# An earlier send-off of one block's row minima in forgetting attention, and another order of weight tiles in the output projection

## The chip, the cores and the metric

The kernel runs on one core of one Trainium2 chip. The metric is the time of one execution on the device, in microseconds (us); less is better. In the views below PE is TensorE (PEld its weight loads), DVE is VectorE, ACT is ScalarE, POOL is GpSimd and SP is SyncE, which only issues transfers here. ACT issues transfers too (ACTq).

## The reference

One inference step of a layer that runs two token mixers on the same input and merges them. What matters here is the attention of the 1024 prompt rows (16 heads of 64, eight pairs of heads), beside a decode step of 8 streams of 16 rows over a cache of 1024 rows, and the output projection with its LayerNorm:

```python
s = jnp.einsum('bqhd,bkhd->bhqk', q, k).astype(jnp.float32) * (A_HEADDIM ** -0.5)
bias = jnp.moveaxis(cq, 1, 2)[..., :, None] - jnp.moveaxis(ck, 1, 2)[..., None, :]
mask = jnp.arange(k.shape[1])[None, :] <= q_pos[:, None]
p = jax.nn.softmax(jnp.where(mask, s + bias, -jnp.inf), axis=-1)
return jnp.einsum('bhqk,bkhd->bqhd', p.astype(v.dtype), v)
...
u = gate_m * jnp.einsum('ble,ed->bld', y_m, w_br_m) + gate_a * jnp.einsum('ble,ed->bld', y_a, w_br_a)
out = jnp.einsum('bld,de->ble', u, w_out)
x_new = layer_norm(DN_ALPHA * x + out, ln_g, ln_b)
```

## The kernel before

The kernel is one long stream of fp32 matmuls on PE. Each operand is split into a high and a low part, and a product is three matmuls (high by high, high by low, low by high; lines 242 to 244). In the attention stage PE computes, for head pair `hp`, the four projections of the pair (v, gate, q, k; a result tile is called `d`), and while it does so the pair before it goes through its attention, a few instructions at a time, in the gaps between projection matmuls. The order of all engines is the order of the code there (a manual schedule). Where each attention step stands is fixed by the list `plan` in the function `pair`: an entry is a position on PE's way through the projections (in ticks of about 1 us), a cost, and the steps that are issued at it.

The keys run down the partitions of a score tile and the queries along it. The 1024 queries are four blocks of 256, j = 0 to 3; block j has 2j+2 key tiles, in `S[j]` (tiles `st_3`, `st_2`). Signs are turned, so that the softmax needs a minimum over the keys. For block 3 and block 2 the steps are:

- `scores` (PE) and the bias on ACT (line 833); `least` folds the minima on DVE; `mins` turns them into columns of the tile `ext` (DVE, lines 856 and 857);
- `share`: PE transposes `ext` (line 862, tile `acmb` for block 3, `acmc` for block 2), DVE reduces the row (`rowmb`, `rowmc`, line 865), SP writes the row to `mn_d` in DRAM (line 876), and when that has landed reads it back, spread over all partitions, into `mb_b` or `mb_c` (line 879). The write and the read are called the trip below;
- `less` subtracts it from the scores on DVE (line 888; block 3 in four pieces that read `mb_b`, block 2 in three that read `mb_c`), `weights` takes the exponential on ACT (line 893);
- `values` multiplies by v on PE into a PSUM tile `o`; DVE then multiplies the gate tile `gs` by it (line 907). Block 3's and block 2's `o` are the same PSUM bank, so `values(2)` on PE waits for line 907 of block 3 on DVE. In DVE's queue that instruction stands behind the three subtractions of block 2.

The decode rows run in the same list: `s_scores` (reads the cache tiles `kc`), `s_weights`, `turn_s` (PE transposes, line 929, copies `PTs` on ACT, lines 930 and 931), `s_values` (reads `vc`). `load` issues one 1 MB cache tile from ACT (line 792) into one of three buffers, in turn; `s_bias` loads `sb` from there too (line 940). An instruction of ACT that issues a load takes its turn in ACT's queue, and the load goes out when that turn has come and its buffer is free.

The output projection (line 1222 on) has eight weight row tiles of `w_out`. Tiles 0 and 1 come through the same ring as all weights before them (`wr`, split into `wh` on ACT, line 224, and `wl` on DVE, line 225). Tiles 2 to 7 (`wor`, `woh`, `wol`, lines 1227 to 1229) lie where buffers of the merge stage lay, so that their loads wait for the last addition of that stage (POOL, line 1210). For each of nine row tiles b and each half n the loop takes k = 0 to 7 in order, three matmuls each (lines 1253 to 1255), into one of eight PSUM banks. Here a scheduler, not the code, sets the order of the instructions on each engine: it takes the matmuls whose inputs it holds to be ready.

Of the kernel before, what the change touches and what calls it, by code (L numbers as in the profile page):

```python
# [147 lines left out]
def trunk_step(ctx: ExitStack, tc: tile.TileContext, I, O):  # L148
    nc = tc.nc
    ve, ac, po, te, sy = nc.vector, nc.scalar, nc.gpsimd, nc.tensor, nc.sync  # L150
# [16 lines left out]
    def bank(name):  # L167
        banks.append(banks.pop(0))
        return pt(banks[-1], name)

    def ch(c):
        return slice(c * CW, (c + 1) * CW)
# [142 lines left out]
    for c in range(NCH):  # L315
        for h in range(4):
            k = slice(2 * h, 2 * h + 2)
# [477 lines left out]
    def pair(hp, r):  # L795
# [223 lines left out]
        def last(i):  # L1019
# [15 lines left out]
            (18.6, 0.2, (share, "b", (3,)), (last, 4)),  # L1035
            (20.0, 3.4, (scores, 2, 2), (s_scores, 0)),
            (23.0, 0.0, (least, 2, 2), (mins, 2, 0, "c")),
            (25.6, 0.0, (s_weights, 0)),
            (26.8, 0.0, (less, 3, 0, 4), (less, 3, 1, 4)),
            (28.4, 0.2, (share, "c", (2,)), (weights, 3, 0, 4), (load, "v", hp, 0, 1), (load, "k", hp, 1, 0), (less, 3, 2, 4), (less, 3, 3, 4)),  # L1040
            (29.4, 0.0, (weights, 3, 1, 4)),
            (30.6, 0.0, (weights, 3, 2, 4)),
            (31.0, 1.2, (turn_s, 0)),
            (32.0, 0.0, (weights, 3, 3, 4)),
            (34.6, 0.0, (less, 2, 0, 3), (less, 2, 1, 3), (less, 2, 2, 3)),
            (35.2, 8.0, (values, 3), (sums, 3), (s_values, 0, 0), (s_values, 0, 1), (s_norm, 0)),
            (36.6, 0.0, (weights, 2, 0, 3)),
            (37.8, 0.0, (weights, 2, 1, 3)),
            (39.2, 0.0, (weights, 2, 2, 3), (load, "k", hp, 1, 1), (s_bias, 1)),
            (45.7, 4.4, (values, 2), (scores, 1, 0), (scores, 1, 1), (least, 1, 0)),  # L1050
            (46.0, 0.0, (load, "v", hp, 1, 0)),
            (49.4, 0.0, (least, 1, 1), (mins, 1, 1, "a")),
# [50 lines left out]
    with tc.manual_schedule():  # L1103
        load("k", 0, 0, 0)
        load("k", 0, 0, 1)
        load("v", 0, 0, 0)
        r = pair_dense(0)
        for hp in range(1, 8):
            flow.start(pair(hp - 1, r))
            r = pair_dense(hp)  # L1110
        flow.start(pair(7, r))
        for j in range(GATES_SSD, GATES_SSD + GATES_FOX):
            gate_dense(j, fp, "kv1", 3)
        flow.drain()
        for fn in lazy.pop("after"):
            fn()
# [100 lines left out]
    wo = []  # L1217
# [16 lines left out]
    for c in range(NCH):  # L1234
        uh = xp.tile([P, 8, CW], F32R, tag=f"xhi{c % 2}", name=f"uh{c}")
        ul = xp.tile([P, 8, CW], F32R, tag=f"xlo{c % 2}", name=f"ul{c}")
        xr = xp.tile([P, 3, D], F32, tag="xlo2", name=f"xres{c}")
        sy.dma_start(xr[:], I["xt"][3 * c * P:(3 * c + 3) * P].rearrange("(j p) d -> p j d", p=P))
        for k in range(8):
            ac.copy(uh[:, k, :], acc[:, k, ch(c)])  # L1240
            ve.tensor_tensor(ul[:, k, :], acc[:, k, ch(c)], uh[:, k, :].bitcast(F32), ALU.subtract)
        for j in range(3):
            b = 3 * c + j
            js = slice(j * P, (j + 1) * P)
            r = op.tile([P, D], F32, tag="r", name=f"r{b}", bufs=3)
            w = 512 if b < 8 else 256
            st = op.tile([P, 4, 6], F32, tag="st", name=f"st{b}", bufs=2)
            mv = op.tile([P, 4], F32, tag="mv", name=f"mv{b}", bufs=2)
            for n in range(D // w):
                ns = slice(w * n, w * n + w)  # L1250
                d = bank(f"out{b}_{n}")
                for k in range(8):
                    te.matmul(d[:, :w], uh[:, k, js], wo[k][0][:, ns], start=(k == 0), stop=False)  # L1253
                    te.matmul(d[:, :w], uh[:, k, js], wo[k][1][:, ns], start=False, stop=False)
                    te.matmul(d[:, :w], ul[:, k, js], wo[k][0][:, ns], start=False, stop=(k == 7))  # L1255
                ve.scalar_tensor_tensor(r[:, ns], xr[:, j, ns], DN_ALPHA, d[:, :w], ALU.mult, ALU.add)
                ve.bn_stats(st[:, n, :], r[:, ns])
            ve.bn_aggr(mv[:, 0:2], st[:, :D // w].rearrange("p n s -> p (n s)"))
            ac.activation(mv[:, 2:3], mv[:, 1:2], AF.Sqrt, bias=epst[:], scale=1.0)
            ve.reciprocal(mv[:, 2:3], mv[:, 2:3])  # L1260
            for n in range(2):
                ns = slice(512 * n, 512 * n + 512)
                ve.scalar_tensor_tensor(r[:, ns], r[:, ns], mv[:, 0:1], gb[:, 0, ns], ALU.subtract, ALU.mult)
                ve.scalar_tensor_tensor(r[:, ns], r[:, ns], mv[:, 2:3], gb[:, 1, ns], ALU.mult, ALU.add)
                sy.dma_start(O["y"][b * P:(b + 1) * P, ns], r[:, ns])
# [86 lines left out]
```

## Time and profile before

| | us |
|---|---|
| median of 3 runs | 2114.12 |
| lowest and highest | 2109.73, 2114.17 |
| profiled execution, its own time | 2111.51 |
| its span, first to last instruction | 2109.7 |
| PE busy in it | 2065.1 |

The profiled execution is 2.6 us below the median. PE is busy for 98% of the span, so that some 45 us can be won by taking waits away from PE, and the other engines count only where PE waits for them.

### The profile page before, as it was taken

Reading aid. Unit: us, or ns where it says so; the run is one execution under the profiler, and the core shown is the slowest. Engines: PE = TensorE matmul, PEld = TensorE weight load, DVE = VectorE, ACT = ScalarE, POOL = GpSimd, SP = SyncE. Lnnn points to the kernel's source line nnn. Section 1 sums busy time; section 2 is a strip of 40 time slices with the busy share of each in tenths; the row PEclk is TensorE's granted clock in tenths of the full one; section 3 lists DMA queues with packets and bytes.
Section 4 is the critical chain, followed back from the end, with each engine's and each line's share of the span. In section 5 each row is a group of like instructions: output and inputs, shape, how many; then the busy total and the mean of one; then the engine's idle time right before and its main releaser. Section 6 shows DMA issues by size and latency. Waiting matters only on the chain.

```text
span 2109.7 us, 36535 instructions
## 1 busy us (share of the span) xinstructions
PE 2065.1 (98%) x14495; PEld 1901.6 (90%) x14495; DVE 1331.3 (63%) x2252; ACT 822.9 (39%) x1662; POOL 625.9 (30%) x789
## 2 busy tenths in 40 slices
PE   8999999999999999999999999999999999999998
PEld 7999989999999998998888889888888999999987
DVE  7578777777777686415776766767767343181365
ACT  3444444443434444325445454454453342020220
POOL 1156564555556463500111121011110012113400
PEclk9999999999999999999999999999999999999999
DMA  5213242423233324333655655545565652153242
GB/s 167 80 54 118 78 135 77 125 76 118 82 117 92 111 83 138 129 136 115 199 169 180 199 169 171 186 164 198 169 203 157 217 193 97 50 184 95 79 175 80
DMA packets 110747, 283.07 MB, mean 134 GB/s; under 512 B 18040, under 2 KB 67184, under 8 KB 100336
## 3 DMA queue, kind: packets, MB, share of 16 engines
q1 hardware_dynamic: 98032, 199.46, 29.6%
q10 hardware_dynamic: 12544, 81.27, 11.6%
q8 instruction: 114, 1.87, 0.4%
q14 instruction: 57, 0.47, 0.1%
HBM read 228.89 MB, written 51.79 MB: 133 GB/s over the span
## 4 chain that ended last, share of the span: by engine, by line
PE 58%; DVE 22%; DMA 10%; ACT 5%; issue 2%; POOL 2%; SPq 0%; ACTq 0%; DVEq 0%; POOLq 0%
PE d L242 14%; PE d L244 13%; PE d L243 13%; DVE st L888 3%; DVE m L605 3%; PE s L828 2%; DMA mn_d<-rowmc 2%; DMA mn_d<-rowmb 2%; DMA ce<-ac_d 2%; PE o L903 2%; PE dq L242 2%; PE dq L243 2%; PE dq L244 2%; PE out L1253 2%; PE out L1255 2%
## 5 line engine op out<-in xcount | busy, mean ns | idle before, releaser
L242 PE MATMUL d<-xh,wh 128*128 128x384 f32 (+1 forms) x2328 | 820.1, 352 | 16.5 <-ACT xh L320 6.4
L244 PE MATMUL d<-xh,wl 128*128 128x384 f32 (+1 forms) x2328 | 781.5, 336 | 0.1
L243 PE MATMUL d<-xl,wh 128*128 128x384 f32 (+1 forms) x2328 | 780.4, 335 | 1.1 <-DVE xl L321 0.9
L242 PEld LDWEIGHTS d<-xh,wh 128*128 128x128 f32 (+1 forms) x2328 | 436.4, 187 | 58.1 <-issue 19.9
L243 PEld LDWEIGHTS d<-xl,wh 128*128 128x128 f32 (+1 forms) x2328 | 436.6, 188 | 4.4 <-DVE xl L321 2.4
L244 PEld LDWEIGHTS d<-xh,wl 128*128 128x128 f32 (+1 forms) x2328 | 435.7, 187 | 1.7 <-DVE wl L225 0.4
L222 POOL TENSOR_TENSOR wl<-wr,wh 128x1024 fp32r<-128x1024 f32 (+1 forms) x58 | 137.7, 2374 | 315.2 <-ACT wh L221 315.2
L221 ACT CAST wh<-wr 128x1024 fp32r<-128x1024 f32 (+1 forms) x73 | 75.8, 1038 | 201.7 <-PE d L243 163.4
L605 DVE TENSOR_SCALAR m<-ce,nacum 128x128 f32<-128x128 f32 x288 | 118.9, 454 | 48.0 <-DMA ce<-ac_d 47.7
L833 ACT ACTIVATE st<-s,ckt 128x256 f32<-128x256 f32 (+1 forms) x320 | 115.0, 465 | 34.2 <-PE s L828 32.1
L893 ACT ACTIVATE st<-st 128x1024 f32<-128x1024 f32 x80 | 84.0, 1061 | 90.9 <-DVE st L888 88.1
L225 DVE SCALAR_TENSOR_TENSOR wl<-wr,wh 128x1024 fp32r<-128x1024 f32 x50 | 61.8, 1235 | 59.7 <-ACT wh L224 59.6
L837 POOL TENSOR_TENSOR st<-st,mask_bf 128x256 f32<-128x256 f32 x64 | 58.7, 937 | 134.7 <-ACT st L833 134.7
L903 PE MATMUL o<-st,vt 128*64 128x256 f32 (+1 forms) x640 | 72.0, 374 | 13.7 <-DVE gs L907 13.3
L903 PEld LDWEIGHTS o<-st,vt 128*64 128x64 f32 x640 | 47.0, 140 | 39.2 <-ACT st L893 18.7
L778 POOL COPY knew<-kf 128x128 f32<-128x128 f32 x8 | 2.3, 290 | 237.6 <-ACT kf L775 237.6
L224 ACT ACTIVATE wh<-wr 128x1024 fp32r<-128x1024 f32 x50 | 52.8, 1056 | 50.6 <-PE d L243 45.9
L819 POOL MEMSET st<- 128x256 f32 x32 | 10.0, 312 | 205.6 <-PE s L828 153.5
L609 DVE TENSOR_TENSOR m<-m,cbm 128x384 f32<-128x384 f32 x96 | 70.2, 780 | 0.6
L607 ACT ACTIVATE ce<-ce 128x384 f32<-128x384 f32 (+1 forms) x96 | 46.8, 487 | 58.1 <-DVE m L605 58.1
L243 PE MATMUL d<-yb0l,wh 128*128 128x384 f32 x192 | 64.1, 334 | 0.0
L243 PE MATMUL d<-yb1l,wh 128*128 128x384 f32 x192 | 64.1, 334 | 0.0
(621 smaller groups left out, 3973.8 us busy)
## 6 DMA issues: line engine op xcount, KB each, us to landing
wr<-in_wt SPq DMA_DIRECT2D x96, 512.0 KB
kc<-in_cache_k ACTq DMA_DIRECT2D x32, 1024.0 KB
vc<-in_cache_v ACTq DMA_DIRECT2D x32, 1024.0 KB
ce<-ac_d SPq DMA_DIRECT2D x96, 192.0 KB
wr<-in_wbr SPq DMA_DIRECT2D x24, 512.0 KB
gate_d<-gate SPq DMA_DIRECT2D x48, 192.0 KB
sb<-cs_d ACTq DMA_DIRECT2D x16, 576.0 KB
yr<-ym_d SPq DMA_DIRECT2D x16, 576.0 KB
```

Source lines behind the costliest of these rows:

```text
L221: ac.copy(hi[:, :cols], raw[:, :cols])
L222: lazy.get("sub", po).tensor_tensor(lo[:, :cols], raw[:, :cols], hi[:, :cols].bitcast(F32), ALU.subtract)
L225: ve.scalar_tensor_tensor(lo[:, :cols], raw[:, :cols], scale, hi[:, :cols].bitcast(F32), ALU.mult, ALU.subtract)
L242: te.matmul(out, wh, xh, start=(k == 0), stop=False)
L243: te.matmul(out, wh, xl, start=False, stop=False)
L244: te.matmul(out, wl, xh, start=False, stop=(k == n - 1))
L605: ve.tensor_scalar(m[:, j, :], ce[:, j * P:(j + 1) * P], nacum[:, b, h:h + 1], 0.0, ALU.add, ALU.min)
L609: ve.tensor_tensor(m[:], m[:], cbms[c][:], ALU.mult)
L833: ac.activation(S[j][:, e, kb, q0:], ps2[:, e, 256 * x + q0:256 * x + 256], AF.Identity, bias=ckt[:, kb, 2 * hp + e:2 * hp + e + 1])
L888: ve.tensor_tensor(w, w, mb[j][:, :, None, :].to_broadcast([P, 2, k1 - k0, 256]), ALU.subtract)
L893: ac.activation(w, w, AF.Exp, scale=-1.0)
L903: te.matmul(o[64 * e:64 * e + 64, 256 * at + q0:256 * at + 256], vt[:, kb, 64 * e:64 * e + 64], S[j][:, e, kb, q0:256], start=(kb == 0), s ...
```

## The change

There are two edits. In `plan` the trip of block 2 (`share "c"`) is issued ahead of block 3's four subtractions instead of between the second and the third. Of the two cache loads that ACT issued between block 3's exponentials, `load v ... 0 1` goes ahead of them (ahead of `s_weights`) and `load k ... 1 0` behind the first exponential of block 2. The other positions move by a tick or less. In the output projection the loop over weight tiles runs 0, 2, 3, 4, 5, 6, 7, 1.

```diff
             (23.0, 0.0, (least, 2, 2), (mins, 2, 0, "c")),
+            (24.0, 0.0, (load, "v", hp, 0, 1)),
             (25.6, 0.0, (s_weights, 0)),
-            (26.8, 0.0, (less, 3, 0, 4), (less, 3, 1, 4)),
-            (28.4, 0.2, (share, "c", (2,)), (weights, 3, 0, 4), (load, "v", hp, 0, 1), (load, "k", hp, 1, 0), (less, 3, 2, 4), (less, 3, 3, 4)),
...
+            (28.8, 0.2, (share, "c", (2,)), (less, 3, 0, 4), (less, 3, 1, 4)),
+            (29.6, 0.0, (weights, 3, 0, 4), (less, 3, 2, 4), (less, 3, 3, 4)),
...
-            (36.6, 0.0, (weights, 2, 0, 3)),
...
+            (37.2, 0.0, (weights, 2, 0, 3), (load, "k", hp, 1, 0)),
...
-                for k in range(8):
+                for k in (0, 2, 3, 4, 5, 6, 7, 1):
                     te.matmul(d[:, :w], uh[:, k, js], wo[k][0][:, ns], start=(k == 0), stop=False)
                     te.matmul(d[:, :w], uh[:, k, js], wo[k][1][:, ns], start=False, stop=False)
-                    te.matmul(d[:, :w], ul[:, k, js], wo[k][0][:, ns], start=False, stop=(k == 7))
+                    te.matmul(d[:, :w], ul[:, k, js], wo[k][0][:, ns], start=False, stop=(k == 1))
```

PE's own order in the attention stage stays as it was, row for row. DVE in the second pair (pair 1), from block 2's minima to block 3's product with the gate, before:

```order
L857 TENSOR_REDUCE ext<-tm_2_11326 128x16
L488 SCALAR_TENSOR_TENSOR gs_11261<-gs_11261,d_0_11268 128x384
L888 TENSOR_TENSOR st_3_11033<-st_3_11033,mb_b 128x2x512 x2
L865 TENSOR_REDUCE rowmc_11367<-acmc_11365 16x32
L888 TENSOR_TENSOR st_3_11033<-st_3_11033,mb_b 128x2x512 x2
L488 SCALAR_TENSOR_TENSOR gs_11261<-gs_11261,d_1_11352 128x384
L888 TENSOR_TENSOR st_2_11180<-st_2_11180,mb_c 128x2x512 x3
L907 TENSOR_TENSOR gs_10354<-gs_10354,o_3_11432 128x256
```

The same stretch of DVE now:

```order
L857 TENSOR_REDUCE ext<-tm_2_11326 128x16
L488 SCALAR_TENSOR_TENSOR gs_11261<-gs_11261,d_0_11268 128x384
L865 TENSOR_REDUCE rowmc_11367<-acmc_11365 16x32
L888 TENSOR_TENSOR st_3_11033<-st_3_11033,mb_b 128x2x512 x4
L488 SCALAR_TENSOR_TENSOR gs_11261<-gs_11261,d_1_11352 128x384
L888 TENSOR_TENSOR st_2_11180<-st_2_11180,mb_c 128x2x512 x3
L907 TENSOR_TENSOR gs_10354<-gs_10354,o_3_11430 128x256
```

The reduction that starts block 2's trip has moved from behind two of the four subtractions to ahead of all four; nothing else has moved on DVE there.

ACT in the same pair, from the decode rows' exponential (line 968) to the load of `sb`, before:

```order
L968 ACTIVATE ps_0_11300,ssum_0_11302<-ps_0_11300,mns_0_11301 128x1152
L487 ACTIVATE gs_11261<-d_0_11268 128x384
L893 ACTIVATE st_3_11033<-st_3_11033 128x2x512
L792 DMA vc_0_1_11373<-in_cache_v 128x2048
L792 DMA kc_1_0_11375<-in_cache_k 128x2048
L893 ACTIVATE st_3_11033<-st_3_11033 128x2x512
L487 ACTIVATE gs_11261<-d_1_11352 128x384
L893 ACTIVATE st_3_11033<-st_3_11033 128x2x512
L930 COPY PTs_0_11395<-tps_0_11396 128x1024
L931 COPY PTs_0_11395<-tns_0_11397 128x128
L893 ACTIVATE st_3_11033<-st_3_11033 128x2x512
L893 ACTIVATE st_2_11180<-st_2_11180 128x2x512 x3
```

The same stretch of ACT now, from one row further up:

```order
L833 ACTIVATE st_2_11180<-s_2_2_11281,ckt 128x128 x2
L792 DMA vc_0_1_11329<-in_cache_v 128x2048
L968 ACTIVATE ps_0_11300,ssum_0_11302<-ps_0_11300,mns_0_11301 128x1152
L487 ACTIVATE gs_11261<-d_0_11268 128x384
L893 ACTIVATE st_3_11033<-st_3_11033 128x2x512 x2
L487 ACTIVATE gs_11261<-d_1_11352 128x384
L930 COPY PTs_0_11392<-tps_0_11393 128x1024
L931 COPY PTs_0_11392<-tns_0_11394 128x128
L893 ACTIVATE st_3_11033<-st_3_11033 128x2x512 x2
L893 ACTIVATE st_2_11180<-st_2_11180 128x2x512
L792 DMA kc_1_0_11496<-in_cache_k 128x2048
L893 ACTIVATE st_2_11180<-st_2_11180 128x2x512 x2
```

The load of `vc` now stands behind block 2's last scores, the load of `kc` behind the first exponential of block 2, and the copies `PTs` ahead of the last two exponentials of block 3 instead of ahead of the last one.

PE at the start of the output projection, from the merge stage's last matmul (`wh121`, `wl121` are tile 0, `wh122`, `wl122` tile 1, `woh2` tile 2; `out0_0` is half 0 of row tile 0), before:

```order
L244 MATMUL d123_2_20335<-yb1h2_19122,wl120_20179 128x384
L1253 MATMUL out0_0_20434<-wh121_20271,uh0_20411 128x512
L1254 MATMUL out0_0_20434<-wl121_20272,uh0_20411 128x512
L1255 MATMUL out0_0_20434<-wh121_20271,ul0_20412 128x512
L1253 MATMUL out0_1_20461<-wh121_20271,uh0_20411 128x512
L1254 MATMUL out0_1_20461<-wl121_20272,uh0_20411 128x512
L1253 MATMUL out0_0_20434<-wh122_20368,uh0_20411 128x512
L1255 MATMUL out0_1_20461<-wh121_20271,ul0_20412 128x512
```

PE now, at the end of its work on tile 0:

```order
L1254 MATMUL out3_1_20679<-wh121_20271,uh1_20629 128x512
L1255 MATMUL out3_1_20679<-wl121_20272,uh1_20629 128x512
L1256 MATMUL out3_1_20679<-wh121_20271,ul1_20630 128x512
L1254 MATMUL out0_0_20434<-woh2_20373,uh0_20411 128x512
L1254 MATMUL out0_1_20461<-woh2_20373,uh0_20411 128x512
L1255 MATMUL out0_0_20434<-wol2_20374,uh0_20411 128x512
```

Before, tile 1 comes up at the 6th matmul, and 41 matmuls with tiles 0 and 1 stand ahead of the first with tile 2; now 24 matmuls stand there, all with tile 0 (eight PSUM banks, three each).

## Rows read from the trace of the kernel before

**Rows 1.** The page, its first part: busy time, share of the span and instructions of each engine.

```profile
PE 2065.1 (98%) x14495; PEld 1901.6 (90%) x14495; DVE 1331.3 (63%) x2252; ACT 822.9 (39%) x1662; POOL 625.9 (30%) x789
```

**Rows 2.** The waits of PE over the whole program: what waited, for what, us in total, times, longest.

```profile
PE o L903 <- DVE gs L907: 13.3, 8, 2.6
...
PE acmc L862 <- DVE ext L857: 2.0, 5, 0.6
PE out L1253 <- ACT wh L224: 1.9, 1, 1.9
PE tns L929 <- DVE rowmc L865: 0.7, 3, 0.3
```

**Rows 3.** The chain of waits in pair 1, from block 3's trip to its product with the gate: start us, us, what.

```profile
1060.41 5.97 DMA mn_d<-rowmb
...
1066.40 3.72 DMA mb_b<-mn_d
...
1070.14 2.36 DVE st L888 x2
...
1072.54 0.31 DVE rowmc L865
...
1072.86 6.57 DMA mn_d<-rowmc
...
1079.45 3.31 DMA mb_c<-mn_d
...
1082.78 3.50 DVE st L888 x3
1086.27 0.34 DVE gs L907
```

**Rows 4.** The timeline of PE at `values(2)` of pairs 1, 4 and 5, the three longest of the eight waits: start us, us, line, operation, tiles, count, in brackets the idle time before and what ended it.

```profile
1086.75 2.60 PE L903 MATMUL o<-st,vt 128*64 128x256 f32 x24 [2.60 <-DVE gs L907]
...
1337.70 4.28 PE L903 MATMUL o<-st,vt 128*64 128x256 f32 x24 [2.24 <-DVE gs L907]
...
1422.39 3.08 PE L903 MATMUL o<-st,vt 128*64 128x256 f32 x18 [2.14 <-DVE gs L907]
```

**Rows 5.** Busy time by stretch, from the start of `values(2)` to the end of the score matmuls behind it, in pairs 1, 4 and 5: stretch, its length, busy us of PE, PEld, DVE, ACT and POOL with their counts, granted TensorE clock (1.00 is 2.4 GHz, 0.50 is 1.2 GHz), DMA share, GB/s.

```profile
1086.75:1090.93 4.18, 4.18 (x49) 3.50 (x49) 4.08 (x4) 2.12 (x4) 0.00 (x0) 1.00 0.71 261
1337.70:1343.53 5.83, 5.83 (x49) 4.48 (x49) 5.58 (x7) 2.65 (x5) 0.31 (x1) 0.71 0.70 237
1422.39:1428.16 5.77, 5.77 (x49) 4.51 (x49) 5.53 (x7) 2.65 (x5) 0.31 (x1) 0.70 0.68 236
```

**Rows 6.** The timeline of all engines in pair 1, columns as in rows 4. The ACT row of line 833 is block 2's last scores, those of line 893 would be exponentials of block 3 (the last is shown); `o` is `values(3)`.

```profile
1061.75 1.35 ACT L833 ACTIVATE st<-s,ckt 128x256 f32<-128x256 f32 x4 [0.36 <-PE s L828]
...
1069.35 0.54 DVE L488 SCALAR_TENSOR_TENSOR gs<-gs,d 128x384 f32<-128x384 f32 x1
1069.58 0.30 PE L862 MATMUL acmc<-ident,ext 128*128 128x128 f32 x1 [0.36 <-DVE ext L857]
...
1071.49 0.33 ACTq L792 DMA_DIRECT2D vc<-in_cache_v  x1
...
1073.56 0.47 ACT L487 ACTIVATE gs<-d 128x384 f32<-128x384 f32 x1
...
1075.44 1.00 ACT L930 COPY PTs<-tps 128x1024 f32<-128x1024 f32 x1
1076.30 3.46 PE L903 MATMUL o<-st,vt 128*64 128x256 f32 x32
...
1076.48 1.07 ACT L893 ACTIVATE st<-st 128x1024 f32<-128x1024 f32 x1
```

**Rows 7.** The chain of waits of the whole program: block 2's write in pair 0, and a write of a row of sums (8 KB) to DRAM at a time when ACT had no cache load under way.

```profile
989.97 5.13 DMA mn_d<-rowmc
...
1468.67 1.69 DMA rc_d<-rows
```

**Rows 8.** The timeline of all engines at the start of the output projection, columns as in rows 4: the merge stage's last addition, the loads of tiles 2 and 3, their conversions on ACT and DVE, and those of tile 7.

```profile
2004.98 1.95 POOL L1210 TENSOR_TENSOR acc<-acc,g 128x384 f32<-128x384 f32 x1 [1.68 <-DVE g L1209]
2006.96 0.81 SPq L1227 DMA_DIRECT2D wor<-in_w_out  x2
...
2011.09 2.23 ACT L1228 ACTIVATE woh<-wor 128x1024 fp32r<-128x1024 f32 x2 [6.28 <-issue]
2012.18 2.39 DVE L1229 SCALAR_TENSOR_TENSOR wol<-wor,woh 128x1024 fp32r<-128x1024 f32 x2 [6.12 <-ACT woh L1228]
...
2025.21 1.06 ACT L1228 ACTIVATE woh<-wor 128x1024 fp32r<-128x1024 f32 x1 [1.35 <-DMA wor<-in_w_out]
...
2026.30 1.22 DVE L1229 SCALAR_TENSOR_TENSOR wol<-wor,woh 128x1024 fp32r<-128x1024 f32 x1 [1.18 <-ACT woh L1228]
```

**Rows 9.** The timeline of PE at the start of the output projection, columns as in rows 4: the first matmul of it, the wait for tile 1, two matmuls that have 24 others between them, and the first with tile 2.

```profile
2001.61 0.39 PE L1253 MATMUL out<-wh,uh 128*128 128x512 f32 x1
...
2004.86 0.50 PE L1253 MATMUL out<-wh,uh 128*128 128x512 f32 x1 [1.94 <-ACT wh L224]
...
2007.38 0.40 PE L1253 MATMUL out<-wh,uh 128*128 128x512 f32 x1
...
2013.07 0.39 PE L1254 MATMUL out<-wl,uh 128*128 128x512 f32 x1
2013.29 1.30 PE L1253 MATMUL out<-woh,uh 128*128 128x512 f32 x5
```

More of the change, by code (lines that the diff above doesn't have):

```diff
@@ L1037, in pair @@
             (23.0, 0.0, (least, 2, 2), (mins, 2, 0, "c")),
+            (24.0, 0.0, (load, "v", hp, 0, 1)),
             (25.6, 0.0, (s_weights, 0)),
-            (26.8, 0.0, (less, 3, 0, 4), (less, 3, 1, 4)),
-            (28.4, 0.2, (share, "c", (2,)), (weights, 3, 0, 4), (load, "v", hp, 0, 1), (load, "k", hp, 1, 0), (less, 3, 2, 4), (less, 3, 3, 4)),
[L1041 to L1046, printed above, removed]
-            (36.6, 0.0, (weights, 2, 0, 3)),
-            (37.8, 0.0, (weights, 2, 1, 3)),
-            (39.2, 0.0, (weights, 2, 2, 3), (load, "k", hp, 1, 1), (s_bias, 1)),
+            (28.8, 0.2, (share, "c", (2,)), (less, 3, 0, 4), (less, 3, 1, 4)),
+            (29.6, 0.0, (weights, 3, 0, 4), (less, 3, 2, 4), (less, 3, 3, 4)),
+            (30.4, 0.0, (weights, 3, 1, 4)),
+            (31.2, 1.2, (turn_s, 0)),
+            (31.8, 0.0, (weights, 3, 2, 4)),
+            (33.2, 0.0, (weights, 3, 3, 4)),
+            (35.4, 0.0, (less, 2, 0, 3), (less, 2, 1, 3), (less, 2, 2, 3)),
+            (35.8, 8.0, (values, 3), (sums, 3), (s_values, 0, 0), (s_values, 0, 1), (s_norm, 0)),
+            (37.2, 0.0, (weights, 2, 0, 3), (load, "k", hp, 1, 0)),
+            (38.4, 0.0, (weights, 2, 1, 3)),
+            (39.8, 0.0, (weights, 2, 2, 3), (load, "k", hp, 1, 1), (s_bias, 1)),
             (45.7, 4.4, (values, 2), (scores, 1, 0), (scores, 1, 1), (least, 1, 0)),
```

## The prediction

> **What bounds the kernel.** I read the page's busy times first: PE is busy for 98% of the span [rows 1], so only time in which PE stands still can be won. The waits of PE say where that is [rows 2]: the largest is `values(2)` (line 903), 13.3 us in eight times, once per head pair, put down to line 907 on DVE; the output projection's wait for weight tile 1 (line 224) is 1.9 us, once. The timeline shows the three longest of the eight: 2.60, 2.24 and 2.14 us [rows 4]. The chain of waits says why they are there [rows 3]. In pair 1 `mb_b` lands (1066.40 + 3.72), DVE does two of block 3's subtractions (2.36), then the reduction to `rowmc` (0.31); the write takes 6.57, the read 3.31, block 2's three subtractions 3.50, and only then comes line 907, which frees the PSUM bank: 1086.27 + 0.34, and PE starts 0.14 later at 1086.75 [rows 3, 4]. So PE's wait is the end of block 2's trip.
>
> The table by stretch adds a cost that the waits do not list [rows 5]. The stretch from `values(2)` to the end of the scores behind it has 49 matmul records in each of three pairs. It takes 4.18 us in pair 1 with a granted clock of 1.00, and 5.83 and 5.77 in pairs 4 and 5 with 0.71 and 0.70: there the clock went to its lower level, 1.2 GHz, for a part of the stretch, after PE had stood for 2.24 and 2.14 us. These two falls cost 1.65 + 1.59 = 3.24 us. The wait of 2.60 us in pair 1 was followed by none.
>
> **First edit, the trip.** `rowmc` needs PE's transpose, done at 1069.58 + 0.30 = 1069.88, and DVE is free of the gate at 1069.35 + 0.54 = 1069.89 [rows 6]. Now it follows at once: about 1069.9 instead of 1072.54, 2.6 us earlier. That covers the longest of the eight waits, 2.60, even if write and read take as long as before. All eight go: **-13.3 us**. With them go the three waits of the `tns` transpose for `rowmc`, 0.7 us [rows 2], since `rowmc` is read that much earlier: **-0.7**. The falls of the clock followed those waits and have no cause left: **-3.24**.
>
> The trip itself should get shorter too. The 2 KB write took 5.13 us in pair 0 and 6.57 in pair 1 [rows 3, 7], right behind ACT's loads of `vc` and `kc` (1071.49 in pair 1, [rows 6]); a write of 8 KB to DRAM with no cache load beside it took 1.69 [rows 7]. Whatever of that comes true is slack and adds nothing to the sum, because another limit is near: line 907 also needs `values(3)` to be done, 1076.30 + 3.46 = 1079.76 in pair 1 [rows 6], and PE would reach `values(2)` at 1086.75 - 2.60 = 1084.15 without waiting. With the old durations `mb_c` lands at about 1070.2 + 6.57 + 3.31 = 1080.1, the subtractions end at 1083.6, line 907 at 1083.9: just in time. With a write of 1.69 there are 4.9 us to spare.
>
> What is late next? Block 3's subtractions start when `rowmc` is done, 1069.9 + 0.31 = 1070.2, against 1070.14 before; all four still end at the same time. ACT does the same four exponentials, one gate and two copies of `PTs`, only in another order, and still ends the last exponential at about 1076.48 + 1.07 = 1077.55. PE needs it for the last quarter of `values(3)`, at 1076.30 + 3/4 x 3.46 = 1078.90 [rows 6]. So **1.35 us of slack** is all there is, and it can be used up by the loads.
>
> **The loads.** ACT now issues `vc` behind block 2's last scores, at 1061.75 + 1.35 = 1063.10 in pair 1 instead of 1071.49 [rows 6]. Its buffer is free by then (the decode scores that read it stand ahead of those rows on PE), so ACT is not held. But it has moved from beside block 2's trip to beside block 3's: `mn_d<-rowmb` is under way from 1060.41 to 1066.38 and `mb_b` from 1066.40 to 1070.12 [rows 3]. No row shows block 3's trip beside a 1 MB cache load. Bounds: nothing from below, since transfers of `sb` and the gate store already run beside that write, which takes 5.97; from above, 2 MB of loads made the small write 6.57 - 1.69 = 4.9 us longer [rows 3, 7], so half of that, 2.4 us, for 1 MB. Up to 1.35 us costs nothing; 2.4 us would stall `values(3)` by 1.05 us in each pair, 8.4 us in all. I take nothing: the load goes out over 3 us before the write lands, so that it meets the write's tail and not a whole leg.
>
> On how the two queues share, the Trainium skill ("DMA: Bandwidth & Descriptors", Queues, rings and completion order) says that each DMA engine takes turns between the queue rows that have work, a packet at a time. By that the trip's transfers are slowed by their turns but not held behind the whole load; the 6.57 us write beside 2 MB does not look like that, so I keep 2.4 us as the upper bound. By the skill alone the sum would be the same, and rival 1 below would be worth about half.
>
> `kc` now goes out behind the first exponential of block 2; the decode scores that read it come at position 54.2 of `plan`, 17 ticks behind. The tile that they read second, and `sb`, go out behind block 2's last exponential as before, which itself comes no later than before. SP's queue is unchanged, and so is POOL's. I cost both at nothing.
>
> **Second edit, the output projection.** The aim is plain: tile 1 is ready late (PE waits 1.94 us at 2004.86, [rows 9]), so it is used last. But tiles 0 and 1 were also the cover for the loads of tiles 2 to 7. These wait for POOL's last addition, 2004.98 + 1.95 = 2006.93, go out at 2006.96, and tile 2 is converted on ACT at 2011.09 + 1.1 = 2012.2 at the earliest [rows 8]. None of this depends on PE. Before, 41 matmuls with tiles 0 and 1 stood ahead of tile 2; at (2013.07 - 2007.38) / 25 = 0.228 us each, with the wait, they end at 2013.29, just when tile 2 is there [rows 9]. Now 24 stand ahead: 2001.61 + 24 x 0.228 = 2007.1. PE then waits until 2012.2: **5.1 us**. I walked the new order through with the end of each conversion from the trace: 0.8 us more for the low part of tile 2 (2012.18 + 1.23 = 2013.41, [rows 8]) and 1.4 us for later tiles up to the low part of tile 7 (2026.30 + 1.22 = 2027.52), in all 7.3 us. The same walk through the old order gives 2.2 us (the trace has 1.94 at its largest wait). Net **+5.1 us**. If the clock falls in that wait of 5.1 us, as it did after 2.14 us, the matmuls behind it are slower, but most of that only fills the 2.2 us of later waits; a walk at half speed for 5.8 us behind the restart ends 1.1 us later, one at half speed for 3.3 us ends no later. Bounds for this edit: +5.1 to +6.2.
>
> The Trainium skill ("TensorE: Matmul & The Clock Gate", HAM oscillation — how this bites in real kernels) says that a wait for data between bursts of matmuls takes the clock back to its lower level, which speaks for the first edit and against the second. This trace agrees for two of the eight waits, 2.24 and 2.14 us, and not for the one of 2.60. By that rule the clock falls in the wait of 5.1 us, which would make the sum up to 1.1 us longer.
>
> **The sum.** -13.3 - 0.7 - 3.24 + 5.1 = -12.1 us. Against the profiled execution's own 2111.5 this is 2099.4. That execution is 2.6 us below the median of the runs; a slower run probably has longer trips or one more fall of the clock, which go as well, but not all of it need be that. I add half of the 2.6: **2100.7 us**.
>
> **Rivals.**
> 1. *Block 3's trip becomes the late one, a little.* The load of `vc` makes `mb_b` 1.35 to 2.4 us later; PE waits before the last key tiles of `values(3)`, up to 8 x 1.05 = 8.4 us: 2101 to 2109. For it: the write beside 2 MB. Against it: the load is mostly through when the read starts.
> 2. *The same, and it takes the whole gain.* If `mb_b` is 3.4 us late in each pair, PE waits 2.05 us there eight times, 16.4 us, and the clock falls twice as before (3.2): 2100.7 + 19.6 = 2120, slower than before. It turns from a gain to a loss at a delay of 1.35 + 12.1/8 = 2.9 us. Against it: that is more than half of what 2 MB did.
> 3. *The output projection keeps its cover.* If the loads of tiles 2 and 3 came earlier, or PE had other work, the edit would save its 1.94 us instead: 2111.5 - 17.2 - 1.9 = 2092. Against it: the order of PE is fixed in the program, and POOL's addition is not touched.
> 4. *The first edit does nothing*, because line 907 waits for something else than the trip. Then only the second is left: 2111.5 + 5.1 = 2116.6. Against it: the 0.14 us between line 907 and `values(2)`, with the trip ending right ahead.
>
> **How the numbers follow.** The forecast has 0.64 (2097 to 2103), rival 1 has 0.20, rival 2 has 0.06, rival 3 has 0.05, rival 4 has 0.05. The range of 2097 to 2109 holds the forecast, the clock's 1.1 us and rival 1. The measurement cannot tell less than 0.2%, 4.2 us, from no change, so faster means below 2109.9. The forecast, rival 3 and nearly all of rival 1 are faster, 0.83 with some room for what I have not seen; the end of rival 1 and part of rival 4 are within 0.2%, 0.10; the rest is slower, 0.07.
>
> **What would show it.** The waits of PE should no longer list `values(2)` behind line 907, nor `tns` behind `rowmc`, and the granted clock in the attention stage should stay at 1.00. In the chain, `rowmc` should stand ahead of the first subtraction of block 3, with a write of 2 to 4 us. At about 1990 in the new trace, 5.4 us behind the output projection's first matmul, PE should stand for about 5 us, with ACT's `woh` named as what ended it. The prediction is wrong if PE waits inside or ahead of `values(3)` for exponentials of block 3, with `mb_b` landing over 1.35 us later against the transpose of `ext` than before.

## The result

| | before | after |
|---|---|---|
| median, us | 2112.46 (4 runs, 2109.73 to 2114.17) | 2096.95 (4 runs, 2094.77 to 2098.63) |
| profiled execution, its own time | 2111.51 | 2095.81 |
| its span | 2109.7 | 2093.9 |

The ratio of the times is 0.9927 (95% interval 0.991 to 0.9944): faster by 15.5 us. The forecast was 2100.7 us, with a range of 2097 to 2109: the median stands at the range's lower edge.

### The profile page after: what moved, and what is told of

The parts are those of the page before. It is cut to its first block, busy times and chain, and to the rows that moved or that the text cites. A ratio compares the mean times of both kernels' runs of the same rounds, so it can differ in the third digit from the quotient of the medians.

```text
span 2093.9 us, 36550 instructions
## 1 busy us (share of the span) xinstructions
PE 2060.3 (98%) x14495; PEld 1900.1 (91%) x14495; DVE 1333.8 (64%) x2252; ACT 820.9 (39%) x1662; POOL 615.8 (29%) x789
## 4 chain that ended last, share of the span: by engine, by line
PE 70%; DVE 16%; DMA 5%; ACT 4%; issue 2%; POOL 2%; SPq 0%; ACTq 0%; DVEq 0%; POOLq 0%
PE d L242 16%; PE d L244 15%; PE d L243 15%; PE o L903 3%; PE s L828 3%; DVE m L605 3%; DMA ce<-ac_d 2%; PE so L978 2%; PE dq L244 2%; PE dq L243 2%; PE dq L242 2%; PE out L1254 2%; PE out L1255 2%; PE out L1256 2%; DVE m L609 1%
## 5 line engine op out<-in xcount | busy, mean ns | idle before, releaser
L837 POOL TENSOR_TENSOR st<-st,mask_bf 128x256 f32<-128x256 f32 x64 | 48.8, 783 | 162.1 <-ACT st L833 162.1
L242 PE MATMUL d<-yb0h,wh 128*128 128x384 f32 x192 | 64.2, 334 | 0.0
L244 PE MATMUL d<-yb0h,wl 128*128 128x384 f32 x192 | 64.2, 334 | 0.0
```

Source lines behind the costliest of these rows:

```text
L242: te.matmul(out, wh, xh, start=(k == 0), stop=False)
L244: te.matmul(out, wl, xh, start=False, stop=(k == n - 1))
```

## The profile after

The first part of the page: busy time, share of the span and instructions of each engine; to be read beside [rows 1].

```profile
PE 2060.3 (98%) x14495; PEld 1900.1 (91%) x14495; DVE 1333.8 (64%) x2252; ACT 820.9 (39%) x1662; POOL 615.8 (29%) x789
```

The waits of PE over the whole program, as in [rows 2].

```profile
PE out L1254 <- ACT woh L1229: 4.5, 1, 4.5
...
PE acmc L862 <- DVE ext L857: 1.2, 3, 0.7
...
PE o L903 <- ACT st L893: 0.9, 2, 0.6
```

The 13.3 us for line 907 and the 0.7 us of `tns` have left the list. In place of 1.9 us for weight tile 1 there are 4.5 us for tile 2. New are two small waits of `values` for an exponential; both are block 1's in the last pair (1595.40 and 1596.81).

The timeline of all engines in pair 1, columns as in [rows 4, 6]:

```profile
1060.22 1.10 SPq L876 DMA_DIRECT2D mn_d<-rowmb  x1
...
1062.65 0.33 ACTq L792 DMA_DIRECT2D vc<-in_cache_v  x1
1065.48 0.33 SPq L879 DMA_DIRECT2D mb_b<-mn_d  x1
1068.90 0.27 PE L862 MATMUL acmc<-ident,ext 128*128 128x128 f32 x1
1069.21 0.30 DVE L865 TENSOR_REDUCE rowmc<-acmc 16x32 f32<-16x128 f32 x1
1069.54 0.32 SPq L876 DMA_DIRECT2D mn_d<-rowmc  x1
1069.69 4.63 DVE L888 TENSOR_TENSOR st<-st,mb_b 128x1024 f32<-128x1024 f32 x4 [0.18 <-DMA mb_b<-mn_d]
...
1071.77 0.32 SPq L879 DMA_DIRECT2D mb_c<-mn_d  x1
...
1075.19 3.50 DVE L888 TENSOR_TENSOR st<-st,mb_c 128x1024 f32<-128x1024 f32 x3 [0.29 <-DMA mb_c<-mn_d]
1075.36 3.46 PE L903 MATMUL o<-st,vt 128*64 128x256 f32 x32
...
1078.87 0.42 DVE L907 TENSOR_TENSOR gs<-gs,o 128x256 f32<-128x256 f32 x1 [0.18 <-PE o L903]
```

`rowmc` follows the transpose at once, 0.31 us behind it instead of 2.96. The write takes 1071.77 - 1069.54 = 2.23 us instead of 6.59 (issue to issue). The three subtractions end at 1078.69, so that line 907 now waits for `values(3)` and not for the trip; PE reaches `values(2)` at 1083.14 without a wait. The trip of block 3 is no longer than before: 5.26 us for the write (before 5.97, [rows 3]), and 9.5 from its issue to the first subtraction (before 9.7). That subtraction starts 0.79 us behind the transpose of `ext` (before 0.56, [rows 3, 6]).

Busy time by stretch, as in [rows 5]: the same 4.18 us from the start of `values(2)` in pairs 1, 4 and 5; then 24 matmuls of the output projection with tile 0, the first 6.1 us with tile 2, and the 6.1 us behind them.

```profile
1083.14:1087.32 4.18, 4.18 (x50) 3.22 (x49) 4.00 (x8) 1.07 (x3) 0.31 (x1) 1.00 0.62 211
1324.64:1328.82 4.18, 4.18 (x50) 3.22 (x49) 4.00 (x8) 1.07 (x3) 0.31 (x1) 1.00 0.62 196
1404.95:1409.13 4.18, 4.18 (x50) 3.22 (x49) 4.00 (x8) 1.07 (x3) 0.31 (x1) 1.00 0.61 197
```

```profile
1980.03:1985.29 5.26, 5.26 (x25) 4.32 (x24) 3.02 (x5) 1.48 (x2) 3.58 (x2) 1.00 0.77 259
1990.22:1996.33 6.11, 6.07 (x13) 4.30 (x14) 2.52 (x3) 2.11 (x2) 0.00 (x0) 0.50 0.85 298
1996.80:2002.90 6.10, 6.10 (x29) 5.04 (x28) 2.76 (x3) 2.12 (x2) 0.00 (x0) 1.00 0.53 172
```

The clock stays at its higher level in the attention stage. It falls to 1.2 GHz behind the wait for tile 2: 13 matmuls in 6.1 us, then 29 in as long. The timeline shows that wait, and what PE waited for:

```profile
1983.42 1.95 POOL L1211 TENSOR_TENSOR acc<-acc,g 128x384 f32<-128x384 f32 x1 [1.68 <-DVE g L1210]
...
1985.40 0.81 SPq L1228 DMA_DIRECT2D wor<-in_w_out  x2
...
1989.11 2.19 ACT L1229 ACTIVATE woh<-wor 128x1024 fp32r<-128x1024 f32 x2 [5.86 <-issue]
...
1990.22 1.22 PE L1254 MATMUL out<-woh,uh 128*128 128x512 f32 x2 [4.54 <-ACT woh L1229]
```

**Where the time went.** PE runs the same 14,495 matmuls in both traces, and up to the output projection in the same order, so the start of each can be subtracted from its start before; where the difference jumps, time was won or lost. The jumps, summed by place, against the forecast:

| place on PE | forecast, us | measured, us |
|---|---|---|
| ahead of the attention stage (same code) | 0 | +1.6 |
| `values(2)`, its wait | -13.3 | -13.9 |
| behind it, the clock | -3.2 | -3.3 |
| transposes of line 929 | -0.7 | -2.3 |
| transpose `acmc` | 0 | -1.3 |
| a projection matmul some 15 us behind `values(2)`, waiting for `ql` (line 761, DVE) | 0 | -2.3 |
| `values(0, 1)`: pairs 0 to 6, pair 7 | 0 | -1.7, +1.5 |
| output projection | +5.1 | +5.7 |
| elsewhere | 0 | +0.1 |
| sum | -12.1 | -15.9 |

The stages ahead of attention start it 0.1 us earlier to 4.5 us later in the ten kernels below, which have the same code there: that row is scatter. So is the row of `acmc`: with the same plan it is -0.3 in attn_only, 0.0 in cover and filled_wait and +0.8 in tile_outer. The +1.5 of pair 7 is 0.0 in attn_only and filled_wait, 0.1 in tile_outer and 0.6 in cover.

## The experiments

Each ratio is against the kernel before, run on the same chip; the intervals are 95%.

| | median, us | ratio |
|---|---|---|
| attn_only | 2090.71 | 0.9895 (0.9882 to 0.9907) |
| outproj_only | 2117.23 | 1.0023 (1.0012 to 1.0034) |
| order_only | 2097.55 | 0.9926 (0.9913 to 0.9939) |
| loads_only | 2096.10 | 0.9919 (0.9908 to 0.9931) |
| cover | 2091.07 | 0.9900 (0.9884 to 0.9916) |
| both_early | 2096.97 | 0.9928 (0.9913 to 0.9943) |
| filled_wait | 2095.64 | 0.9923 (0.9908 to 0.9938) |
| gate_first | 2107.40 | 0.9984 (0.9975 to 0.9993) |
| tile_outer | 2089.04 | 0.9882 (0.9867 to 0.9897) |
| tile_outer_vc_late | 2088.89 | 0.9878 (0.9862 to 0.9895) |

### The two edits apart: attn_only and outproj_only

attn_only is the changed kernel with `for k in range(8)` in the output projection, outproj_only the kernel before with `for k in (0, 2, 3, 4, 5, 6, 7, 1)`.

> The attention edit alone, with the output projection in the order of before. Aligning PE's 14,495 matmuls of the two traces one by one gives -23.2 us within the attention stage and +5.7 in the output projection. If the two edits are independent, this kernel takes about 2112.5 - 22 = 2090 us (2088 to 2092), 6 us less than the changed kernel. Rival: the later pace of PE and the loads of the merge and output stages hang together, so that a part of the gain is lost without the second edit; then 2093 or more.

> The output projection's edit alone, with the plan of before. If tile 1 was cover for the conversion of tile 2, this is slower than before by 5.1 to 6.2 us, 2117.6 to 2118.7, with PE standing for 4.5 us behind its 24th matmul of the projection. Rival: the wait of 4.5 us is an effect of the earlier attention stage (POOL's last addition not being earlier by as much as PE); then this kernel is within 2 us of before, or faster by the 1.9 us of the wait for tile 1.

The first is 22.9 us faster than before, the second 3.6 us slower by the medians. In its trace outproj_only loses 5.56 us in the output projection and has the wait (4.9 us for `woh`); it had one fall of the clock less than before in the attention stage. The medians alone do not add up to the change closely (-22.9 + 3.6 = -19.3 against -15.5), the stages do: attention -23.7 in attn_only and -23.2 in the changed kernel, output projection +5.6 in outproj_only and +5.7. So the two edits are independent, one a gain of some 23 us and the other a loss of 5 to 6, and the rival explanations (a shared gain, a wait caused by the earlier attention) fall.

### The two halves of the first edit: order_only and loads_only

```diff
 order_only, against attn_only
-            (24.0, 0.0, (load, "v", hp, 0, 1)),
-            (29.6, 0.0, (weights, 3, 0, 4), (less, 3, 2, 4), (less, 3, 3, 4)),
+            (29.6, 0.0, (weights, 3, 0, 4), (load, "v", hp, 0, 1), (load, "k", hp, 1, 0), (less, 3, 2, 4), (less, 3, 3, 4)),
-            (37.2, 0.0, (weights, 2, 0, 3), (load, "k", hp, 1, 0)),
+            (37.2, 0.0, (weights, 2, 0, 3)),
 loads_only, against before
+            (24.0, 0.0, (load, "v", hp, 0, 1)),
-            (28.4, 0.2, (share, "c", (2,)), (weights, 3, 0, 4), (load, "v", hp, 0, 1), (load, "k", hp, 1, 0), (less, 3, 2, 4), (less, 3, 3, 4)),
+            (28.4, 0.2, (share, "c", (2,)), (weights, 3, 0, 4), (less, 3, 2, 4), (less, 3, 3, 4)),
-            (36.6, 0.0, (weights, 2, 0, 3)),
+            (36.6, 0.0, (weights, 2, 0, 3), (load, "k", hp, 1, 0)),
```

> Against attn_only, the two cache loads stand behind block 3's first exponential again, and block 2's minima still go off ahead of the subtractions. If the earlier start of the trip is what takes the waits away, this is within 2 us of attn_only (2088 to 2093), with the write of rowmc at 2 to 3 us, since it is through before the loads go out, and the read longer by up to 3 us, which its slack covers. If the cleared transfers are what matters, waits for the product with the gate come back in several pairs and the kernel takes 2095 to 2105 us.

> The two loads moved as in the change, while block 2's minima still go off between the second and the third subtraction; output projection as before. If the earlier start is needed, the waits stay for the most part, and the kernel takes 2100 to 2110 us. If a trip without loads beside it is enough by itself, the write takes 2.2 us instead of 5 to 6.6, the end of the trip is 3 to 4 us earlier, and the eight waits go: 2091 to 2095 us, 1 to 3 us above attn_only, because the transpose behind rowmc still waits (some 2 us in all).

Each half alone gives 16 to 17.5 us of the 22.9; in the attention stage order_only wins 17.2 us, loads_only 16.2 and attn_only 23.7. I had thought that one of them would do. The median of order_only (2097.55) lies in its rival's range, and that of loads_only (2096.10) 1 us above the better of its two. The timeline of order_only shows what is left over; in pair 7:

```profile
1558.27 0.32 SPq L876 DMA_DIRECT2D mn_d<-rowmc  x1
...
1559.94 0.33 ACTq L792 DMA_DIRECT2D vc<-in_cache_v  x1
1560.37 0.39 ACTq L792 DMA_DIRECT2D kc<-in_cache_k  x1
1560.51 0.32 SPq L879 DMA_DIRECT2D mb_c<-mn_d  x1
...
1570.59 3.50 DVE L888 TENSOR_TENSOR st<-st,mb_c 128x1024 f32<-128x1024 f32 x3 [7.34 <-DMA mb_c<-mn_d]
...
1574.68 4.28 PE L903 MATMUL o<-st,vt 128*64 128x256 f32 x24 [2.77 <-DVE gs L907]
```

The write has gone ahead of the loads and is short (2.24 us), but the read now stands behind them: 1570.59 - 1560.51 = 10.08 us, and the wait of `values(2)` and a fall of the clock are back. In the other pairs the read takes 5.2 to 7.1 us, and only pair 3 waits (0.34): the waits came back in two pairs, not in several. In loads_only the write takes 1.33 us in seven pairs (3.26 in pair 1), the read 3.3, and all eight waits are gone. There PE waits for the transposes instead, more than before ([rows 2]): for `tns` 1.5 us, and for `acmc` 3.0 (2.14 of it in the last pair, with a fall of the clock behind it that cost some 1.5; attn_only has 1.2 us of these waits and tile_outer 2.6). So a write without loads ahead of it is worth as much as the earlier start, and only both together clear the waits of `values(2)` and of `tns`.

### The place in DVE's queue: gate_first

```diff
 against before
-            (34.6, 0.0, (less, 2, 0, 3), (less, 2, 1, 3), (less, 2, 2, 3)),
-            (35.2, 8.0, (values, 3), (sums, 3), (s_values, 0, 0), (s_values, 0, 1), (s_norm, 0)),
+            (35.2, 8.0, (values, 3), (less, 2, 0, 3), (less, 2, 1, 3), (less, 2, 2, 3), (sums, 3), (s_values, 0, 0), (s_values, 0, 1), (s_norm, 0)),
```

> The kernel before with one thing changed: on DVE the product with the gate (line 907) that frees the PSUM bank stands ahead of block 2's three subtractions. Loads and trips as before. If PE's wait is one for a place in DVE's queue, it becomes a wait for block 2's exponentials: 1.2 us in pair 1 instead of 2.60, 3 us in all instead of 13.3, at most one fall of the clock; 2097 to 2101 us. If the bank is really freed late by values(3), nothing changes: 2112 to 2115.

It gives 4.0 us (the medians, 2111.40 for before on this chip; the profiled executions differ by 6.6), under a third of what I expected. The waits behind line 907 are gone, and so are the falls of the clock, but two other waits stand there, in pair 1:

```profile
1085.00 1.08 PE L903 MATMUL o<-st,vt 128*64 128x256 f32 x8 [0.97 <-ACT st L893]
...
1101.40 0.44 PE L242 MATMUL d<-xh,wh 128*128 128x384 f32 x1 [0.78 <-DVE ql L761]
```

The first is the expected one, only larger: later exponentials hold up `values(2)` as well, by 0.3 us and less at a time. By the matmuls' starts it wins 11.4 of the 17.2 us that it wins in the changed kernel (13.9 and 3.3 for the clock), so that the exponentials cost 5.7 and not 3. The second I had missed: PE waits 0.78 us for `ql` in each of seven pairs, and by the matmuls' starts these places cost 5.1 us more than before. DVE's queue is late behind the trip, and a PE that no longer waits at `values(2)` meets it 15 us later. Only an earlier end of the trip makes DVE itself earlier.

### The slack of block 3's trip: both_early

```diff
 against attn_only
-            (24.0, 0.0, (load, "v", hp, 0, 1)),
+            (24.0, 0.0, (load, "v", hp, 0, 1), (load, "k", hp, 1, 0)),
-            (37.2, 0.0, (weights, 2, 0, 3), (load, "k", hp, 1, 0)),
+            (37.2, 0.0, (weights, 2, 0, 3)),
```

> attn_only with both cache loads issued at the place of the first, ahead of the decode rows' exponential, beside block 3's trip. By the prediction's slack of 1.35 us in values(3) and by what 2 MB did to block 2's trip (3 to 5 us), mb_b lands 1.5 to 4 us later and PE waits inside values(3) in every pair: 8 to 24 us above attn_only, 2098 to 2114. If block 3's trip is bound by the stores on SP's queue and not by the loads, nothing changes: 2089 to 2093.

It is 5.9 us slower than cover, below, on the same chip, which has the plan of attn_only (in the attention stage -18.8 us against -22.8). The timeline of pair 1:

```profile
1071.59 0.30 PE L862 MATMUL acmc<-ident,ext 128*128 128x128 f32 x1
...
1074.48 4.63 DVE L888 TENSOR_TENSOR st<-st,mb_b 128x1024 f32<-128x1024 f32 x4 [2.25 <-DMA mb_b<-mn_d]
...
1080.73 1.91 PE L903 MATMUL o<-st,vt 128*64 128x256 f32 x16 [0.74 <-ACT st L893]
```

The subtractions start 2.89 us behind the transpose instead of 0.79, so 2.1 later, and `values(3)` waits 0.74 for an exponential: the slack is 1.36 us. The write takes 5.46 us there (5.26 in the changed kernel), but the subtractions start 6.33 us behind the read's issue instead of 4.20: the second load falls on the read. Over the eight pairs `values(3)` costs 5.0 us more, less than the 8 to 24 that I expected. Rival 1 of the prediction is real; it needs the second load.

### The output projection: filled_wait, cover, tile_outer

```diff
 filled_wait, against after
+                for _ in range(7 if (b, n) == (3, 1) else 0):
+                    te.matmul(d[:, :w], uh[:, 0, js], wo[0][0][:, ns], start=True, stop=False)
+                    te.matmul(d[:, :w], uh[:, 0, js], wo[0][1][:, ns], start=False, stop=False)
+                    te.matmul(d[:, :w], ul[:, 0, js], wo[0][0][:, ns], start=False, stop=True)
                 for k in (0, 2, 3, 4, 5, 6, 7, 1):
 cover, against attn_only (row_tiles issues the three matmuls of each k)
...
+            for k in range(2):
+                for b in range(4):
+                    for n in range(2):
+                        if k == 0:
+                            heads[b, n] = bank(f"out{b}_{n}")
+                        row_tiles(heads[b, n], b, slice(512 * n, 512 * n + 512), (k,))
...
 tile_outer, against cover
-            for k in range(2):
-                for b in range(4):
+            for k in range(8):
+                for terms in ((0, 2), (1,)) if k == 2 else ((0, 1, 2),):
+                    for b in range(4):
...
```

> The changed kernel with 21 more matmuls of tile 0 in the eighth PSUM bank (seven times the same three, the sum started anew each time), so that PE works through most of the wait for tile 2 and its clock has no reason to fall there. If the fall (0.50 for 6.8 us) costs time, this kernel is faster than the changed one although it does more: up to 1.1 us faster by the walk of the prediction, 2095 to 2096.5. If the slow stretch only fills later waits, it is the same within 0.5 us; if the matmuls are in the way, slower.

> The attention edit with another output projection: tile 0 over all eight PSUM banks, then tile 1 over all eight, then tiles 2 to 7 bank by bank. If tile 1 is late by itself and tile 2 is late because the cover ahead of it is too short, both waits go: tile 1 is wanted 5.5 us after the first matmul (it was ready at 3.3), tile 2 at 10.9 (ready at 10.6). Against attn_only the wait of 1.94 us and the clock's fall behind it (1.44 us) go: 2087 to 2089 us. If the order within a bank is not what counts, it is within 1 us of attn_only, 2090 to 2092.

> As cover, but the first eight PSUM banks take all eight tiles tile by tile, so that one tile gives 24 matmuls (5.5 us) of work and tile k is wanted 5.5 k us after the first matmul; of tile 2 the high part is used over all banks before the low part. In the trace of cover the tiles are there at 10.6 (tile 2), 16.4 (tile 4) and 25 us (tile 7). If the arrival of tiles 2 to 7 is what holds the output projection at 2.1 to 2.4 us of lost time in before and in cover alike, it falls under 0.3 us here: 2.0 to 2.3 us below cover, and 3.5 below attn_only, at 2087 to 2088.5 us. If the evacuation of eight banks at once makes PE wait instead, it is no faster than cover.

The output projection is read from its first matmul on: by how much a matmul starts later than at the full pace of 0.2275 us each. At its last matmul of full width (row tile 8 has narrower ones) this is 2.07 us in before, 7.79 after, 3.52 in attn_only, 2.32 in cover and -0.28 in tile_outer.

filled_wait is within the scatter of the changed kernel (ratio 0.9923 against 0.9927). The clock no longer falls there, but with 21 matmuls more (4.78 us) it is 2.63 us late, 7.41 in all, against 7.79. The fall took 3.0 us from the second matmul behind the restart on; without it PE does the last four of the added matmuls behind the wait (0.9 us) and then waits for tile 5 (1.1 us), so that all but 0.4 us is lost again.

cover removes the wait for tile 1 and yet is no better than before in this stage, 0.25 us longer. The waits of PE that it has:

```profile
PE out L1254 <- ACT woh L1229: 0.9, 1, 0.9
PE out L1255 <- DVE wol L1230: 0.6, 1, 0.6
```

The timeline shows which tiles these are: ACT converts tiles 2 and 3 (the first row), 4 and 5, and the longer wait ends with the fourth conversion.

```profile
1989.58 2.21 ACT L1229 ACTIVATE woh<-wor 128x1024 fp32r<-128x1024 f32 x2 [6.30 <-issue]
1990.67 2.37 DVE L1230 SCALAR_TENSOR_TENSOR wol<-wor,woh 128x1024 fp32r<-128x1024 f32 x2 [6.14 <-ACT woh L1229]
...
1995.38 1.06 ACT L1229 ACTIVATE woh<-wor 128x1024 fp32r<-128x1024 f32 x1 [3.60 <-DMA wor<-in_w_out]
...
1998.38 1.06 ACT L1229 ACTIVATE woh<-wor 128x1024 fp32r<-128x1024 f32 x1 [1.93 <-DMA wor<-in_w_out]
...
1999.49 0.50 PE L1254 MATMUL out<-woh,uh 128*128 128x512 f32 x1 [0.86 <-ACT woh L1229]
```

Tiles 2 and 5 are now the late ones. The load of tile 5 goes out at 1993.07, when DVE has done tile 3 (1990.67 + 2.37), since the loads take turns in two staging buffers (`wor`); a third buffer was not tried. Against attn_only nothing was gained in the ratios; the 1.9 us for tile 1 cannot be won as long as tiles 2 and 5 are wanted as early. tile_outer wants a tile every 5.5 us, and PE has no wait left in the output projection: -2.35 us against before in that stage, and 2.6 below cover, where I expected 2.0 to 2.3. Its median is 0.5 us above the expected range, and its ratio, the lowest but one of all, beats the changed kernel's and before's but overlaps with those of attn_only and cover.

### What a load does to a small write: tile_outer_vc_late

```diff
 against tile_outer
-            (62.6, 0.0, (load, "v", hp, 1, 1)),
-            (66.4, 1.2, (turn_s, 1)),
+            (66.4, 1.2, (turn_s, 1), (load, "v", hp, 1, 1)),
```

> As tile_outer, with the cache load of vc that stands ahead of block 1's trip (position 62.6) put behind the copies of the second decode rows (66.4). If that load is what makes block 1's write 3.8 to 6.0 us, the write falls to under 3 us in the pairs, and the wait ahead of the exponentials of block 1 in the last pair (0 to 1.5 us) goes; 0 to 1.5 us below tile_outer. If the vc tile is then late for the decode product behind values(1), PE waits there and it is slower by 1 us a pair or more.

The timeline of tile_outer in pair 1, and then of tile_outer_vc_late:

```profile
1098.39 0.33 ACTq L792 DMA_DIRECT2D vc<-in_cache_v  x1
...
1099.65 0.32 SPq L876 DMA_DIRECT2D mn_d<-rowma  x1
1103.62 0.32 SPq L879 DMA_DIRECT2D mb_a<-mn_d  x1
```

```profile
1101.86 0.32 SPq L876 DMA_DIRECT2D mn_d<-rowma  x1
1103.21 0.32 SPq L879 DMA_DIRECT2D mb_a<-mn_d  x1
...
1107.73 0.34 ACTq L792 DMA_DIRECT2D vc<-in_cache_v  x1
```

The write takes 1.35 us instead of 3.97 (1.34 to 1.51 in the eight pairs, against 3.71 to 4.97). The time is the same within the scatter (0.9878 against 0.9882), since nothing waited for that trip; the last pair of tile_outer had no such wait to lose.

## Why the prediction was right

**The trip.** All eight waits went (-13.9 for -13.3 forecast), with `rowmc` at 1069.21 right behind the transpose, and line 907 at the end of `values(3)`. That an earlier start was enough by itself was nearly right: order_only still has 3.1 us of these waits, because the read meets the loads there. I let the earlier `rowmc` and the shorter trip add nothing beyond the waits that the list names, and here the working was wrong. Three places won 5.6 us that the sum did not have:

- Line 929 won 2.3 us and not 0.7. The list has three of these waits, the starts show six, of 0.2 to 0.5 us. They belong to the earlier start: order_only wins 2.4 there, and loads_only, where `rowmc` is as late as before, loses 0.6.
- The place of `ql` won 2.3 us and `values(0, 1)` of pairs 0 to 6 won 1.7. They belong to the end of the trip, behind which DVE's queue gets earlier: loads_only, with the shorter trip alone, wins 2.3 and 1.5 there, order_only 1.4 and 0.9. gate_first shows the link for `ql`: when PE's wait goes and DVE stays late, that wait grows by 5 us.

**The clock.** Both falls of the attention stage went, -3.3 for -3.24. That there were two to win hangs on the execution: outproj_only, with the attention stage of before, had one.

**The loads.** The bound of 2.4 us for 1 MB was right in size: the middle one of block 1's writes in the eight pairs is 3.83 us with the load ahead of it (tile_outer) and 1.35 without (tile_outer_vc_late), 2.5 us less. It did not fall on block 3's trip, where the load goes out 2.4 us behind the write: its first subtraction is 0.2 us later against the transpose in pair 1; 2 MB make it 2.1 later and use up the slack, which is 1.36 us as worked out. The value taken, nothing, was right for `values(3)`. In the last pair the load ahead of block 1's trip went out 1.41 us ahead of the write instead of 0.67, the write took 5.98 us instead of 4.79, and PE waited 1.5 us for exponentials: a cost that was not in the sum. In attn_only the load was 1.41 us ahead too, but the write took 4.63 and nothing waited; what makes this difference stays open.

On how queues share, the Trainium skill ("DMA: Bandwidth & Descriptors", Queues, rings and completion order) says that an engine drains a whole packet of some 9 to 17 descriptors before it turns to another row. I had read it as turns of single pieces. A load of 1 MB is 128 rows of 8 KB, so 8 pieces on each of 16 engines, an estimate from its shape: the whole load would fit one turn. The writes of 1.35 and 3.8 us behind no load and 1 MB fit that; the 5.1 to 6.6 behind 2 MB do not tell whether one load went first or both. The view of the DMA queues in tile_outer agrees for 1 MB. From the write's issue at 1099.65 to 1102.40 it has 111 of the load's 128 pieces (ACT's queue, q10) and none of the write, which then is through at 1103.62:

```profile
DMA packets 111, 0.91 MB, mean 331 GB/s; under 512 B 0, under 2 KB 0, under 8 KB 0
...
q10 hardware_dynamic: 111, 0.91, 79.5%
```

No run changed the size of the pieces, so that the turns themselves are argued and not shown.

**The output projection.** The wait came 5.65 us behind the stage's first matmul (forecast 5.4), of 4.5 us for 5.1. It ran from 1985.7 to 1990.2; the forecast's 1990 was meant for its start, and the stage began 4 to 5 us earlier than that took for granted. With the clock's fall behind it the stage lost 5.7 us, between the two walks (5.1 and 6.2). filled_wait shows that the fall cost 0.4 us and not 3. That tile 1 was cover is shown by outproj_only. The 1.9 us of rival 3 do not come with more cover alone (cover); they come when the tiles behind it are wanted later too (tile_outer).

**The rivals.** Rivals 2, 3 and 4 did not come; rival 1 came only when a second load was added. Against the profiled execution the sum was 3.6 us too slow (2099.4, and 2095.81 measured): attention won 7.6 us more than forecast (the 5.6 above, 1.3 of scatter at `acmc`, 0.7 in the forecast's own terms), of which the last pair's wait (1.5), the output projection (0.6) and the scatter ahead of attention (1.6) took back 3.7. That these errors are of opposite sign is luck: without the 3.7 us the time would lie below the range. The step that was mis-sized is the one that let the earlier `rowmc` and the shorter trip add nothing beyond the listed waits.

## What to carry to other kernels

Ask of an edit whether it makes the late queue itself earlier, so that its later waits go too, or only changes who waits, so that they come back further on as in gate_first. Issue bulk loads behind a small transfer that others wait for, not ahead of it, and where a read follows the write, behind that read too: in order_only they stood between the two, and the read took up to 10 us. Before a late input is moved to the end of a loop, ask what it covered: here tiles 0 and 1 were the time in which tile 2 was fetched.

## What I had not expected of the hardware

The wait of 1.93 to 1.94 us for tile 1 is the same in six kernels (before, attn_only, order_only, loads_only, both_early, gate_first). The granted clock fell behind it in three of them and not in the others. Here are the stretches behind that wait, first of attn_only, then of before:

```profile
1981.74:1985.40 3.66, 3.66 (x9) 2.90 (x10) 1.20 (x2) 0.00 (x0) 1.94 (x1) 0.54 0.86 301
```

```profile
2004.86:2008.50 3.64, 3.64 (x15) 2.84 (x16) 1.20 (x2) 0.00 (x0) 1.95 (x1) 1.00 0.91 320
```

Nine matmuls against fifteen in the same time; the stage ends 1.45 us later in attn_only (3.52 against 2.07). In outproj_only the clock fell behind a wait of 2.62 us at `values(2)` in pair 4 (0.66 in the 5 us behind it) and not behind one of 2.58 in pair 1 (1.00). So a wait of about 2 us leaves it open whether the clock falls, and the same stage can differ by that from one kernel to another. What decides it was not tried. The Trainium skill ("TensorE: Matmul & The Clock Gate", HAM oscillation — how this bites in real kernels) tells of waits for data between bursts that bring the clock down; the wait of 4.54 us agrees, those of 1.94 agree in half of the cases.
